# A fused trunk on one core: the four products into the residual take the weights as the moving operand, and the residual is kept with a token to a partition

## The chip, the core and the metric

The kernel is one program on one of the eight cores of a Trainium2 chip. The metric is the device time of one execution in microseconds (us); the time of a kernel is the median of its runs. Of the core's engines five matter here: PE multiplies matrices, DVE, ACT and POOL compute elementwise, and the queue of SP issues nearly all loads from memory.

## What is computed

The batch is one sequence of 256 tokens of width 2048, in float32. Two layers follow each other; each has a mixer and an MLP, and each of these reads the residual `h` through a norm with a scale and a shift that a conditioning vector `c` gives, and adds its result back through a gate:

```python
for i in range(2):
    mod = (silu(c) @ w_mod[i] + b_mod[i])          # 6 x 2048 numbers
    sh1, sc1, g1, sh2, sc2, g2 = split(mod, 6)
    u = rmsnorm(h, norm_mix_g[i]) * (1 + sc1) + sh1
    mix = conformer_conv(u) if i == 0 else mamba2(u)
    h = h + g1 * mix
    u = rmsnorm(h, norm_mlp_g[i]) * (1 + sc2) + sh2
    h = h + g2 * ((relu(u @ w1[i]) ** 2) @ w2[i])  # 2048 -> 8192 -> 2048
return rmsnorm(h, final_norm_g)
```

`conformer_conv` is a product to 4096 columns (pw1), a gate, a causal convolution of 31 taps per channel, a layer norm and a product 2048 to 2048 with a bias (pw2). `mamba2` is a product to 10,304 columns, a short convolution, a scan over two chunks of 128 tokens, a norm and a product 4096 to 2048 (wout). So four products go into the residual: pw2, the w2 of layer 0, wout, and the w2 of layer 1.

## The kernel before

**Tiles.** Activations lie with a channel to a partition: a tile is 128 channels by 256 tokens. The residual `h` is four tiles of [128, 4, 256]. Only within the last MLP it is turned round: `to_rows` transposes `h` into two tiles of [128 tokens, 2048] (`ht`).

**Products.** Weights arrive in tiles of 1 MB (512 rows by 512 columns, `load_w`, three buffers). For precision each is split, in two halves of 128x1024 numbers: ACT casts a half to the high part `wh` (L292), DVE computes the rest `wl` (L293); activations are split the same way and stored side by side (512 columns: 256 high, 256 low). Two ways of multiplying stand in the program:

- `block` (L311 on): the weight is the stationary operand, the activation moves. Per 128x128 piece of weight there is one matmul over 512 columns (`wh` with both parts) and one over 256 (`wl` with the high part): 512 matmuls for four tiles. In the form `single` there are three of 256 columns instead. One *block* is 512 output columns from 2048 input rows, hence four weight tiles.
- `block_t` (L333 on): the activation is stationary, the weight moves, always 512 columns: per 128 rows of weight three matmuls for each half of the tokens (L350 to L352). The result has a token to a partition. Before the change only the w2 of layer 1 uses it.

`outer` runs the first three blocks of an MLP's w1 together, with the norm's output made on the way.

**Into the residual.** `into_acc` adds the partial results of a w2 chunk (there are four chunks `c` of 2048 hidden channels) into accumulators on DVE and ACT; `into_h` multiplies by the gate, a number per partition, and adds to `h` on DVE (L627), and ACT squares the result (L443) for the norm that follows. `rstd_bcast` sums the squares over partitions by PE (L419), takes the root and spreads the result over all partitions by PE (L433). `modulate` then makes the next input `u` with DVE and ACT.

**The conditioning.** The 24,576 numbers of `mod` are 192 dot-product jobs (*gemvs*): a tile of w_mod of 1 MB (`wm<-wmT`) is loaded by SP, and DVE multiplies it by `silu(c)` and sums it (L247, SCALAR_TENSOR_TENSOR `wm`); after each fourth, POOL adds the bias (L255), which completes one tile `mod` of 4 columns. From the first MLP on, the tiles go through a ring of two buffers `wm`. They are streamed beside the products: `pump(n)` starts n jobs of a list at each weight tile, by the lists `RATE_...`; `need(layer, seg)` starts at once whatever of a segment is still in the list. The gate of the MLP is the segment G2. In `mlp(0)` the list is G2 of layer 0 first, then the segments of layer 1.

**What sets the order.** All loads of weights and of w_mod are on the queue of SP and are held in the order in which the program starts them (`stream`). On the engines the order is made by a scheduler from the program's order and priorities: splits of a weight tile are drawn `ahead` by a number of instructions. Small jobs (`todo`) are generators; `step`, called within the products, advances them by one. They use the two PSUM banks `ms`, the products use the six banks `mm`.

Of the kernel before, what the change touches and what calls it, by code (L numbers as in the profile page):

```python
# [15 lines left out]
P = 128  # L16
# [68 lines left out]
def layout(inp):  # L85
# [26 lines left out]
    for l, s, g in PE_GROUPS:  # L112
# [3 lines left out]
        "fg": np.ascontiguousarray(a["final_norm_g"].reshape(1, D)),  # L116
        "xT": np.ascontiguousarray(a["x"][0].T.reshape(4, 4, P, T).transpose(0, 2, 1, 3)),
# [27 lines left out]
class Trunk:  # L145
# [40 lines left out]
    def prologue(self):  # L186
        nc, a = self.nc, self.a
        self.h = [self.b("h", [P, 4, T]) for _ in range(4)]
# [8 lines left out]
        for g in range(4):  # L197
            nc.scalar.dma_start(out=self.h[g], in_=a["xT"][g])
# [134 lines left out]
    def block_t(self, src, rhs, evac):  # L333


        banks = [self.bank(self.mm, "mm") for _ in range(2)]
        mm = self.nc.tensor.matmul
        for g in range(4):
            w = self.load_w(src[g])
            with self.tc.high_priority(self.ahead):  # L340
                parts = self.split_w(w)
            for i, (wh, wl) in enumerate(parts):
                last = g == 3 and i == 1
                order = [(q, k) for q in range(2) for k in range(2)] if last else [
                    (q, k) for k in range(2) for q in range(2)]
                for q, k in order:
# [3 lines left out]
                    mm(banks[q], lhsT=hi, rhs=wh[:, k, :], start=g == 0 and t == 0, stop=False)  # L350
                    mm(banks[q], lhsT=hi, rhs=wl[:, k, :], start=False, stop=False)  # L351
                    mm(banks[q], lhsT=lo, rhs=wh[:, k, :], start=False, stop=g == 3 and t == 3)  # L352
                    if last and k:
                        evac(q, banks[q])
                self.step()
                self.step()

# [88 lines left out]
    def modulate(self, r, layer, sc, sh, g):  # L446

        ug = self.b("u", [P, 4, 2 * T], F32R)
        for t in range(4):
            m = self.t("nrm", [P, T], bufs=2)  # L450
            self.nc.vector.scalar_tensor_tensor(
                out=m, in0=self.h[g][:, t, :], scalar=self.mod_tile(layer, sc, g)[:, t:t + 1],
                in1=r, op0=ALU.mult, op1=ALU.mult)
            self.split_x(ug, t, m, self.mod_tile(layer, sh, g)[:, t:t + 1])
        return ug


    def conformer(self):
        nc, a = self.nc, self.a
        ss = []  # L460
        for g in range(4):
            for t in range(4):
                ss = self.square_sum(ss, self.h[g][:, t, :])
# [4 lines left out]
        def make_u(g):  # L468
            for t in range(4):
                m = self.t("nrm", [P, T], bufs=2)  # L470
                nc.vector.scalar_tensor_tensor(
                    out=m, in0=self.h[g][:, t, :], scalar=self.mod_tile(0, SC1, g)[:, t:t + 1],
# [92 lines left out]
        native([(b, a["pw1"][b]) for b in range(FIRST)], u, glu, before=before)  # L565
# [49 lines left out]
    def into_h(self, st, b, gate, after=None):  # L615
# [9 lines left out]
        def evac(j, parts):  # L625
# [3 lines left out]
            if after:  # L629
                after(4 * b + j, h(j))  # L630
# [427 lines left out]
```

## Time and profile before

| | |
|---|---|
| time, median of 3 runs | 2635.68 us (2634.64 to 2639.17) |
| the profiled execution | 2639.67 us, of which the span of the profile is 2637.9 us |
| PE busy | 2531.5 us, 96% of the span |
| DVE busy | 2038.0 us, 77% |
| ACT busy | 1358.4 us, 51% |
| POOL busy | 193.1 us, 7% |
| read from memory | 652.83 MB |

All times below are in us from the start of the span. The stages lie so: the first norm and pw1 with the convolution to about 345, pw2 to 453, MLP of layer 0 to 1189 (its w1 chunk 0 from 461 to 555.7, its w2 chunk 0 from 555.7 to 646.3), mamba to 1704, wout to 1896, MLP of layer 1 to 2626, the last norm to the end. PE busy counts pipelined matmuls, so it says that PE had work, not that it ran at its peak; the granted clock (PEclk) is the share of full speed that PE was given.

### The profile page before, as it was taken

The page shows a single profiled execution, that of the slowest core. Times are in us where ns is not written, and L with a number is a line of the kernel's source. Part 1 is how long each engine was busy: PE and PEld are TensorE (multiplying, and loading weights), DVE is VectorE, ACT ScalarE, POOL GpSimd, SP SyncE. Part 2 cuts the span into 40 slices and gives each one's busy share as a digit, 9 for nine tenths or more (in the row PEclk, how much of TensorE's full clock was granted, in tenths as well). Part 3 has the DMA queues.
Part 4 walks back from the last instruction along what each step waited for, and adds up shares of the span by engine and source line. Part 5 has one row for each costly group of instructions (what it writes and reads, how often), then busy time and mean ns, then how long its engine had stood idle before and what let it go on. Part 6 is the DMA issues. An engine that isn't in the chain of part 4 may idle for free.

```text
span 2637.9 us, 36706 instructions
## 1 busy us (share of the span) xinstructions
PE 2531.5 (96%) x14359; PEld 2189.4 (83%) x14359; DVE 2038.0 (77%) x2738; ACT 1358.4 (51%) x2141; POOL 193.1 (7%) x189
## 2 busy tenths in 40 slices
PE   4799879999999999999999999999999999999998
PEld 3688469988888888898888888888997888888886
DVE  7799988987888888888877777888865565565565
ACT  2288654454443434446877766744454344443443
POOL 0023310000000000000000000000000101101000
PEclk9899889999999999999999999999999999999999
DMA  9866659788888888874655555688655555555554
GB/s 406 341 251 254 260 215 354 303 318 323 317 313 330 324 321 311 327 302 164 221 183 184 166 194 182 217 298 316 249 187 176 191 192 191 191 181 196 185 190 143
DMA packets 92591, 657.40 MB, mean 249 GB/s; under 512 B 10465, under 2 KB 10465, under 8 KB 14465
## 3 DMA queue, kind: packets, MB, share of 16 engines
q1 hardware_dynamic: 88274, 640.73, 66.3%
q0 software_dynamic: 3136, 10.59, 1.3%
q10 hardware_dynamic: 1008, 3.75, 0.4%
q8 instruction: 112, 1.84, 0.3%
q14 instruction: 61, 0.50, 0.1%
HBM read 652.83 MB, written 2.20 MB: 248 GB/s over the span
## 4 chain that ended last, share of the span: by engine, by line
PE 86%; DVE 9%; DMA 2%; issue 2%; ACT 1%; POOL 0%; ACTq 0%; SPq 0%; DVEq 0%; POOLq 0%
PE mm L300 69%; PE mm L352 4%; PE mm L351 4%; PE mm L350 4%; DVE taps L503 3%; DVE taps L506 2%; DMA hid<-wmT 2%; DVE hid L247 1%; PE mm L546 1%; DVE wm L247 1%; PE ms L972 1%; DVE wl L293 0%; PE ms L433 0%; DMA h<-xT 0%; PE ms L419 0%
## 5 line engine op out<-in xcount | busy, mean ns | idle before, releaser
L300 PE MATMUL mm<-u,wh 128*128 128x512 f32 (+1 forms) x4544 | 1378.2, 366 | 4.0 <-ACT u L401 1.9
L292 ACT CAST wh<-w 128x1024 fp32r<-128x1024 f32 x768 | 806.7, 1050 | 1027.4 <-PE mm L300 732.8
L293 DVE TENSOR_TENSOR wl<-w,wh 128x1024 fp32r<-128x1024 f32 x768 | 942.4, 1229 | 461.0 <-ACT wh L292 455.6
L300 PE MATMUL mm<-u,wl 128*128 128x256 f32 x3840 | 1083.4, 283 | 0.1
L300 PEld LDWEIGHTS mm<-u,wh 128*128 128x128 f32 x4544 | 815.3, 191 | 149.5 <-issue 3.4
L300 PEld LDWEIGHTS mm<-u,wl 128*128 128x128 f32 x3840 | 731.5, 191 | 3.8 <-issue 1.7
L300 PE MATMUL mm<-hid,wh 128*128 128x512 f32 (+1 forms) x1344 | 455.6, 389 | 2.8 <-DVE acc L644 2.8
L300 PE MATMUL mm<-hid,wl 128*128 128x256 f32 x1280 | 360.4, 282 | 0.0
L247 DVE SCALAR_TENSOR_TENSOR wm<-wm,scb 128x2048 f32<-128x2048 f32 x135 | 308.9, 2288 | 2.3 <-DMA wm<-wmT 2.3
L300 PEld LDWEIGHTS mm<-hid,wh 128*128 128x128 f32 x1344 | 249.0, 189 | 60.5 <-DVE acc L644 3.1
L546 PE MATMUL mm<-u,w 128*128 128x256 f32 x1024 | 230.2, 389 | 21.3 <-ACT u L474 21.3
L300 PEld LDWEIGHTS mm<-hid,wl 128*128 128x128 f32 x1280 | 242.6, 190 | 0.2 <-issue 0.2
L546 PEld LDWEIGHTS mm<-u,w 128*128 128x128 f32 x1024 | 199.8, 196 | 51.5 <-ACT u L474 23.0
L352 PE MATMUL mm<-wh,hid 128*128 128x512 f32 x512 | 199.9, 391 | 0.0
L350 PE MATMUL mm<-wh,hid 128*128 128x512 f32 x512 | 199.9, 390 | 0.0
L351 PE MATMUL mm<-wl,hid 128*128 128x512 f32 x512 | 199.5, 390 | 0.0
L497 ACT ACTIVATE taps<-u,par 128x256 f32<-128x256 f32 x360 | 148.6, 499 | 19.6 <-DVE u L488 10.5
L255 POOL TENSOR_TENSOR mod<-mod,par 128x4 f32<-128x4 f32 x48 | 52.5, 1094 | 1080.3 <-DVE wm L247 880.5
L247 DVE SCALAR_TENSOR_TENSOR hid<-hid,scb 128x2048 f32<-128x2048 f32 x49 | 113.9, 2329 | 14.9 <-ACT scb L202 11.2
L352 PEld LDWEIGHTS mm<-wh,hid 128*128 128x128 f32 x512 | 96.2, 188 | 19.7
L350 PEld LDWEIGHTS mm<-wh,hid 128*128 128x128 f32 x512 | 96.2, 188 | 19.7
L351 PEld LDWEIGHTS mm<-wl,hid 128*128 128x128 f32 x512 | 96.2, 188 | 19.5
(197 smaller groups left out, 1623.9 us busy)
## 6 DMA issues: line engine op xcount, KB each, us to landing
w<-w SPq DMA_DIRECT2D x256, 1024.0 KB, 4.9
wm<-wmT SPq DMA_DIRECT2D x137, 1024.0 KB, 7.2
w<-win SPq DMA_DIRECT2D x80, 1024.0 KB, 4.9
hid<-wmT SPq DMA_DIRECT2D x55, 1024.0 KB, 8.3
w<-pw SPq DMA_DIRECT2D x48, 1024.0 KB, 5.1
w<-wout SPq DMA_DIRECT2D x32, 1024.0 KB, 6.3
acc<-ac_d POOLq DMA_DIRECT2D x16, 512.0 KB, 7.2
h<-xT ACTq DMA_DIRECT2D x4, 512.0 KB, 13.1
```

Source lines behind the costliest of these rows:

```text
L247: nc.vector.scalar_tensor_tensor(out=w, in0=w, scalar=1.0, in1=self.scb, op0=ALU.mult, op1=ALU.mult, accum_out=m[:, i:i + 1])
L255: nc.gpsimd.tensor_tensor(out=m, in0=m, in1=self.col("b_mod", (layer * 6 + seg) * NT + 4 * kg, 4), op=ALU.add)
L292: nc.scalar.copy(out=wh, in_=w[:, s, :])
L293: nc.vector.tensor_tensor(out=wl, in0=w[:, s, :], in1=wh.bitcast(F32), op=ALU.subtract)
L300: mm = lambda out, lhsT, rhs, **kw: self.nc.tensor.matmul(out, lhsT=lhsT, rhs=rhs, skip_group_check=True, **kw)
L350: mm(banks[q], lhsT=hi, rhs=wh[:, k, :], start=g == 0 and t == 0, stop=False)
L351: mm(banks[q], lhsT=hi, rhs=wl[:, k, :], start=False, stop=False)
L352: mm(banks[q], lhsT=lo, rhs=wh[:, k, :], start=False, stop=g == 3 and t == 3)
L497: nc.scalar.activation(out=p4[:, q, :], in_=vp[:, k + q:k + q + T], func=AF.Identity, scale=self.col("w_dw", ct * TAPS + k + q), bias=self ...
L503: nc.vector.tensor_add(wide, wide, p4)
L506: nc.vector.scalar_tensor_tensor(out=o, in0=vp[:, k:k + T], scalar=self.col("w_dw", ct * TAPS + k), in1=o, op0=ALU.mult, op1=ALU.add)
L546: nc.tensor.matmul(o, lhsT=w[:, t, j * P:(j + 1) * P], rhs=rhs[g][:, t, :], start=g == 0 and t == 0 and j < 2, stop=g == 3 and t == 3, ski ...
```

## The change

- `h` is two tiles [128 tokens, 2048] from the start. They are loaded from a second copy of the input with tokens as rows (`a["x"]`), by the queue of SP among the loads of pw1. The transposed input stays for the first norm alone (`xT`, in the buffers `acc`).
- pw2, the w2 of layer 0 and wout use `block_t` too. `block_t` takes a list of weight tiles, a `pump`, and banks that are kept open over two calls: of wout the first half of the rows is done for three blocks (six open banks), then the second half for these, then both halves of the fourth.
- `into_rows` does the evacuation for all four: DVE multiplies a bank by the gate as rows and POOL adds it to `h`; where the residual is complete after it (pw2, wout, the last chunk of a w2), DVE adds and ACT squares and sums.
- `gate_rows` makes the gate as rows in all partitions: `row` multiplies the gate column, broadcast as stationary operand, by the identity, 4 calls of 128 columns for each 512 numbers, into a bank `ms` that ACT copies out. In pw2 a second such set carries gate times bias, and DVE adds it to `h`. In the MLP of layer 0 `need(layer, G2)` and `gate_rows` now stand after the w1 chunk 0, ahead of the w2 chunk 0.
- A norm (`normed`) is a sum of the squares' sums, root and reciprocal for each token, DVE and ACT scale the rows into two tiles, and `modulate` transposes them back by PE, 32 transposes of 128x128 in a norm, and applies scale and shift from PSUM on ACT and DVE. `to_rows` and, for the three norms concerned, `rstd_bcast` are gone.

```diff
-    def block_t(self, src, rhs, evac):
-        banks = [self.bank(self.mm, "mm") for _ in range(2)]
+    def block_t(self, srcs, rhs, evac, pump=None, banks=None, done=True):
+        first = banks is None
+        banks = banks or [self.bank(self.mm, "mm") for _ in range(2)]
...
+    def normed(self, sq):
+        nc = self.nc
+        r = self.t("rcol", [P, 2])
+        nc.vector.reduce_sum(out=r, in_=sq, axis=mybir.AxisListType.X)
+        nc.scalar.activation(out=r, in_=r, func=AF.Sqrt, scale=1.0 / D, bias=self.eps)
+        nc.vector.reciprocal(r, r)
+        x = [self.b("hid", [P, D]) for _ in range(2)]
+        for g in range(4):
+            s = slice(g * 512, (g + 1) * 512)
+            for q in range(2):
+                if g and q:
+                    nc.scalar.mul(out=x[q][:, s], in_=self.h[q][:, s], mul=r[:, q:q + 1])
+                else:
+                    nc.vector.tensor_scalar_mul(out=x[q][:, s], in0=self.h[q][:, s], scalar1=r[:, q:q + 1])
+        return x
+
+    def modulate(self, x, layer, sc, sh, g):
...
+        for i in range(2):
+            ps = self.bank(self.ms, "ms")
+            for t in range(2):
+                ct = 4 * g + 2 * i + t
+                for q in range(2):
+                    nc.tensor.transpose(ps[:, t * T + q * Q:t * T + (q + 1) * Q],
+                                        x[q][:, ct * P:(ct + 1) * P], self.ident)
+            for t in range(2):
...
+                nc.scalar.activation(out=ug[:, k, :T], in_=v, func=AF.Identity, scale=c, bias=o)
+                m = self.t("nrm", [P, T], bufs=2)
+                nc.vector.tensor_scalar(out=m, in0=v, scalar1=c, scalar2=o, op0=ALU.mult, op1=ALU.add)
+                nc.vector.tensor_tensor(out=ug[:, k, T:], in0=m, in1=ug[:, k, :T].bitcast(F32), op=ALU.subtract)
...
+        for q in range(2):
+            self.stream(self.h[q], a["x"][q])
...
-            self.block(a["pw2"][b], v, self.into_h(st, b, gate), pump=pump, single=True)
+        self.todo.append(self.gate_rows(0, G1, gb))
+        for b in range(4):
+            self.block_t(a["pw2"][b], v, self.into_rows(b, True), pump=pump)
...
+    def row(self, ps, cols):
+        for j in range(4):
+            self.nc.tensor.matmul(ps[:, j * P:(j + 1) * P], lhsT=cols[:, j:j + 1].broadcast_to([P, P]),
+                                  rhs=self.ident, start=True, stop=True)
...
-            if layer == 1:
-                for b in range(4):
-                    self.block_t(a["w2"][layer, c, b], hid, self.into_rows(b, c == 3))
-                continue
+            if c == 0:
+                self.need(layer, G2)
+                self.todo.append(self.gate_rows(layer, G2))
             for b in range(4):
-                if c == 3:
-                    self.need(layer, G2)
-                ev = self.into_h(st, b, gate, after) if c == 3 else self.into_acc(st, b, c == 0)
-                self.block(a["w2"][layer, c, b], hid, ev, pump=pump, single=c == 3 and b == 3)
+                self.block_t(a["w2"][layer, c, b], hid, self.into_rows(b, c == 3, finish), pump=pump)
...
-        for b in range(4):
-            self.block(a["wout"][0, b], self.out_hl[:4], self.into_acc(st, b, True), pump=pump)
+        half = lambda i, b, **kw: self.block_t(a["wout"][i, b], self.out_hl[4 * i:4 * i + 4], self.into_rows(b, True),
+                                               pump=pump, **kw)
+        open_ = [half(0, b, done=False) for b in range(3)]
         while self.todo:
             self.step()
-        self.need(1, G1)
-        for b in range(4):
-            self.block(a["wout"][1, b], self.out_hl[4:], self.into_h(st, b, gate), pump=pump, single=b == 3)
-        self.need(1, SC2, SH2)
+        for b in range(3):
+            half(1, b, banks=open_[b])
+        half(1, 3, banks=half(0, 3, done=False))
+        self.need(1, SC2, SH2, G2)
```

How the order of instructions moves is shown at three places, all at the passage from the w1 to the w2 of chunk 0 in the MLP of layer 0.

The queue of SP, before: `w_564` and `w_570` are the last two weight tiles of w1, `w_588` and `w_594` the first two of w2; each `wm` is one tile of w_mod.

```order
L277 DMA w_564_4088<-w 128x2048
L277 DMA wm_4090<-wmT 128x2048
L277 DMA w_570_4133<-w 128x2048
L277 DMA w_588_4208<-w 128x2048
L277 DMA wm_4210<-wmT 128x2048
L277 DMA w_594_4253<-w 128x2048
```

The queue of SP, now: `w_570` is again the last tile of w1, `w_596` the first of w2.

```order
L279 DMA w_570_3788<-w 128x2048
L279 DMA wm_3859<-wmT 128x2048
L279 DMA wm_3862<-wmT 128x2048
L279 DMA wm_3866<-wmT 128x2048
L279 DMA wm_3870<-wmT 128x2048
L279 DMA wm_3873<-wmT 128x2048
L279 DMA wm_3876<-wmT 128x2048
L279 DMA wm_3880<-wmT 128x2048
L279 DMA wm_3884<-wmT 128x2048
L279 DMA wm_3887<-wmT 128x2048
L279 DMA wm_3890<-wmT 128x2048
L279 DMA w_596_3896<-w 128x2048
```

Ten loads of w_mod, which are the rest of segment G2, now stand between the last tile of w1 and the first of w2; in the queue before there is none at this place. In return ten loads of w_mod are gone from the end of wout.

DVE, now, at the same passage: `wm` rows are gemvs, `a` and `hid` rows the rest of the evacuation of the last w1 block, the `wl` row the first split of w2.

```order
L249 SCALAR_TENSOR_TENSOR wm_3866,mod_3868<-wm_3866,scb 128x2048
L411 TENSOR_TENSOR hid_3818<-a_3844,hid_3818 128x256
L720 SCALAR_TENSOR_TENSOR a_3855<-lo_3852 128x256
L249 SCALAR_TENSOR_TENSOR wm_3870,mod_3868<-wm_3870,scb 128x2048
L411 TENSOR_TENSOR hid_3818<-a_3855,hid_3818 128x256
L249 SCALAR_TENSOR_TENSOR wm_3873,mod_3868<-wm_3873,scb 128x2048
L249 SCALAR_TENSOR_TENSOR wm_3876,mod_3868<-wm_3876,scb 128x2048
L249 SCALAR_TENSOR_TENSOR wm_3880,mod_3882<-wm_3880,scb 128x2048
L249 SCALAR_TENSOR_TENSOR wm_3884,mod_3882<-wm_3884,scb 128x2048
L249 SCALAR_TENSOR_TENSOR wm_3887,mod_3882<-wm_3887,scb 128x2048
L249 SCALAR_TENSOR_TENSOR wm_3890,mod_3882<-wm_3890,scb 128x2048
L295 TENSOR_TENSOR wl_3903<-w_596_3896,wh_3902 128x1024
```

The first two of the ten gemvs (`wm_3859`, `wm_3862`) come just ahead of the evacuation of the last w1 block; the third, the first row here, stands behind the reads of all four banks of that block, and the first split of w2 behind the tenth. Before, the first tile of w2 was split ahead of that evacuation.

PE, now, at the start of the w2 chunk 0: `ms` rows are `gate_rows`, `mod` the finished gate columns.

```order
L302 MATMUL mm_3654<-u_3377,wh_3794 128x512
L302 MATMUL mm_3654<-u_3377,wl_3795 128x256
L654 MATMUL ms_3930<-ident,mod_3701 128x128 x4
L654 MATMUL ms_3949<-ident,mod_3868 128x128 x4
L654 MATMUL ms_3955<-ident,mod_3882 128x128 x4
L358 MATMUL mm_3894<-wh_3902,hid_3453 128x512
L358 MATMUL mm_3895<-wh_3902,hid_3453 128x512
L359 MATMUL mm_3894<-wl_3903,hid_3453 128x512
```

Three of the four groups of gate rows stand between the last matmul of w1 and the first of w2; before, the two followed each other directly.

197 lines of the change are left out of this document (81 added, 116 removed).

## The prediction

> **What bounds the kernel now.** I read the page first, the engines' busy time and the chain of waits:
>
> ```profile
> PE 2531.5 (96%) x14359; PEld 2189.4 (83%) x14359; DVE 2038.0 (77%) x2738; ACT 1358.4 (51%) x2141; POOL 193.1 (7%) x189
> PE 86%; DVE 9%; DMA 2%; issue 2%; ACT 1%; POOL 0%; ACTq 0%; SPq 0%; DVEq 0%; POOLq 0%
> ```
>
> PE has work nearly always and holds 86% of the chain. So a matmul less counts in full, and so does every new wait of PE. Which holds where is read from the windows by stage (busy time per engine, then granted clock, share of the DMA engines, GB/s):
>
> ```profile
> core 0: us, PE busy (x) PEld busy (x) DVE busy (x) ACT busy (x) POOL busy (x), PEclk, DMA share, GB/s
> 357.00:400.00 43.00, 42.18 (x325) 41.89 (x326) 39.72 (x70) 27.02 (x47) 1.12 (x1) 0.91 0.73 276
> 400.00:453.40 53.40, 53.40 (x446) 53.21 (x444) 47.99 (x56) 21.95 (x28) 2.63 (x4) 1.00 0.95 361
> 453.40:461.40 8.00, 3.30 (x22) 2.88 (x21) 6.54 (x12) 4.08 (x8) 0.00 (x0) 0.71 0.78 295
> 461.40:555.70 94.30, 94.30 (x705) 91.31 (x706) 85.76 (x113) 46.60 (x72) 6.53 (x5) 0.97 0.81 305
> 555.70:646.30 90.60, 90.60 (x515) 78.61 (x514) 72.81 (x82) 40.38 (x54) 3.35 (x3) 1.00 0.87 321
> 1098.50:1189.40 90.90, 90.90 (x577) 81.73 (x575) 79.59 (x103) 39.67 (x52) 3.75 (x5) 1.00 0.80 303
> 1704.00:1804.90 100.90, 98.10 (x572) 84.42 (x571) 86.86 (x118) 47.02 (x66) 4.59 (x5) 0.98 0.81 301
> 1804.90:1895.80 90.90, 90.90 (x577) 81.77 (x575) 80.63 (x101) 38.09 (x46) 3.35 (x3) 1.00 0.80 305
> 1895.80:1902.20 6.40, 4.08 (x29) 3.60 (x29) 4.37 (x11) 3.63 (x8) 0.00 (x0) 0.88 0.48 172
> 1902.00:1999.00 97.00, 97.00 (x732) 94.04 (x731) 58.85 (x89) 50.35 (x80) 0.00 (x0) 0.97 0.48 163
> 1999.00:2093.30 94.30, 93.09 (x418) 74.92 (x417) 52.04 (x64) 37.70 (x42) 11.45 (x6) 1.00 0.56 190
> 2183.70:2270.80 87.10, 87.10 (x386) 72.13 (x386) 47.64 (x50) 35.62 (x38) 10.60 (x6) 1.00 0.57 193
> ```
>
> Each product into the residual fills PE: in both halves of pw2 (357 to 453.4), in the w2 chunks of layer 0 (555.7 to 646.3 is chunk 0, 1098.5 to 1189.4 chunk 3) and in wout (1704 to 1895.8) the busy time is the window or close to it. The last row is a w2 chunk of layer 1, which already uses `block_t`: 87.1 us for the work that takes `block` 90.6. PE is not full in the passages between stages, 453.4 and 1895.8, where the norm's chain runs.
>
> **The change part by part: the four products.** `block` and `block_t` are compared by these rows: four blocks cost 90.6, 90.9 where one of them is `single`, and 87.1 in the new form. The gain is 90.6 - 87.1 = 3.5 us for each of the w2 chunks 0 to 2 of layer 0, 10.5; chunk 3 gives 90.9 - 87.1 = 3.8; wout 3.5 and 3.8 in its two halves (100.9 holds other small matmuls, which stay), 7.3. In pw2 all four blocks are single, each 0.3 dearer by the difference above: 90.6 + 1.2 - 87.1 = 4.7. Sum **-26.3**. It depends on DVE keeping up. In layer 0 and wout it is busy 73 to 87 us of a chunk; in pw2 39.72 + 47.99 = 87.7, which is more than the new 87.1. There the gain is the least sure, from 0 to 4.7.
>
> **Gate rows and `to_rows`.** The nearest rows are those of `to_rows` in the MLP of layer 1:
>
> ```profile
> L717 PE MATMUL ms<-diag,ones 128*128 128x128 f32 x32 | 7.2, 306 | 1.2 <-DVE diag L716 1.2
> L705 PE MATMUL ms<-ident,h 128*128 128x128 f32 x32 | 5.3, 293 | 0.7 <-ACT wm L706 0.7
> ```
>
> The 16 float32 calls of the gate (two records each, x32) fall into the window 1999.0 to 2093.3, which is 94.3 - 87.1 = 7.2 us longer than one without: 0.45 us a call with the wait for DVE, each alone among other matmuls. The 32 transposes fall into 1902 to 1999, 97.0 - 94.3 = 2.7 longer than the same stage of layer 0: 0.084 each. By their own row, 5.3 + 0.7, it would be 0.19. A gate call now is of the same size, but four follow each other and none waits for a diagonal from DVE. So its cost lies between two such records, 2 x 0.084 = 0.17, and 0.45; I take 0.25, nearer the first, because transposes also come in fours. pw2 has 32 calls: 8.0. The MLP of layer 0 has 16; four stand before the last w1 block, 1.0, and twelve in the stall below. wout has 16: 4.0. In layer 1 16 calls, 4.0, replace the 7.2 + 2.7 of `to_rows`: -5.9. Sum **+7.1** (+4 to +20). The ACT copies and the eight DVE additions of pw2 lie beside PE, but the second set of a group waits for a bank that DVE frees. If that cover fails, 8 x 0.69 = 5.5 us are added.
>
> **Transposes of the norms.** 32 in each of three norms, 0.084 to 0.19: 2.7 to 6.0 a norm; I take 3.3, since the difference of windows is wall time. PE is full from the first matmul of each stage on, so nothing hides them. Sum **+10** (8 to 18).
>
> **The norm's chain.** How long the new chain is, the end of the kernel shows, which has it already:
>
> ```profile
> 2625.90 0.69 DVE L734 TENSOR_TENSOR t<-mm,h 128x512 f32<-128x512 f32 x1
> 2626.63 0.69 DVE L738 TENSOR_TENSOR wm<-wm,t 128x512 f32<-128x512 f32 x1
> 2627.24 0.68 DVE L740 TENSOR_TENSOR wm<-wm,h 128x512 f32<-128x512 f32 x1
> 2627.35 0.63 ACT L739 ACTIVATE t<-wm 128x512 f32<-128x512 f32 x1 [0.64 <-DVE wm L738]
> 2628.72 0.15 DVE L1026 TENSOR_REDUCE rcol<-mom 128x2 f32<-128x8 f32 x1
> 2628.91 0.29 ACT L1027 ACTIVATE rcol<-rcol,eps 128x2 f32<-128x2 f32 x1 [0.83 <-DVE rcol L1026]
> 2629.24 0.17 DVE L1028 RECIPROCAL rcol<-rcol 128x2 f32<-128x2 f32 x1 [0.36 <-ACT rcol L1027]
> ```
>
> From the last matmul to the reciprocal 3.5 us, of which L740's multiplication by the last norm's weight delays some 0.6 that the middle norms lack; then one scaling of a half's 512 columns, 0.7 like L740, the first transposes at half clock, some 0.9, and an ACT pass of 0.5. That is 5 to 6 us against 8.0 at 453.4 and 6.4 at 1895.8. **-2** for the three (-5 to +3).
>
> **The ten gemvs.** This decides. The order of the queue of SP shows ten loads of w_mod between the last w1 tile and the first w2 tile of chunk 0, and the ring has two buffers: each load waits for the gemv two before it. What such a load and its work cost, and when they stood there before:
>
> ```profile
> L247 DVE SCALAR_TENSOR_TENSOR wm<-wm,scb 128x2048 f32<-128x2048 f32 x135 | 308.9, 2288 | 2.3 <-DMA wm<-wmT 2.3
> L255 POOL TENSOR_TENSOR mod<-mod,par 128x4 f32<-128x4 f32 x48 | 52.5, 1094 | 1080.3 <-DVE wm L247 880.5
> w<-w SPq DMA_DIRECT2D x256, 1024.0 KB, 4.9
> wm<-wmT SPq DMA_DIRECT2D x137, 1024.0 KB, 7.2
> ```
> ```profile
> 521.44 0.42 SPq L277 DMA_DIRECT2D wm<-wmT  x1
> 527.20 0.43 SPq L277 DMA_DIRECT2D wm<-wmT  x1
> 532.80 6.15 SPq L277 DMA_DIRECT2D w<-w  x2
> ```
> ```profile
> 534.03 2.29 DVE L247 SCALAR_TENSOR_TENSOR wm<-wm,scb 128x2048 f32<-128x2048 f32 x1
> 539.52 2.29 DVE L247 SCALAR_TENSOR_TENSOR wm<-wm,scb 128x2048 f32<-128x2048 f32 x1
> 549.93 2.52 DVE L293 TENSOR_TENSOR wl<-w,wh 128x1024 fp32r<-128x1024 f32 x2
> 555.14 0.75 DVE L393 TENSOR_TENSOR lo<-mm,lo 128x256 f32<-128x256 f32 x2
> 556.48 2.28 DVE L247 SCALAR_TENSOR_TENSOR wm<-wm,scb 128x2048 f32<-128x2048 f32 x1
> ```
>
> In the clock of before: the two gemvs ahead of the ten end at 536.3 and 541.8, so loads 1 and 2 issue then. In DVE's order gemv 1 stands behind the last split of w1, which at 549.93 is the first of the two and stood behind a gemv that now comes after it; so it starts at about 548.5, and gemvs 1 and 2 end at 550.8 and 553.1. Loads 3 and 4 land 5 us later, but gemv 3 stands behind the reads of the last w1 block's four banks, whose last matmul ends at 555.7. It runs from about 556.6 to 558.9. Only then load 5 issues. From there the ring alone paces: a load of 4.9 and a gemv of 2.3 make 7.3 us for each buffer, two buffers by turns. Load 5 at 559.0, 7 at 566.3, 9 at 573.6; load 6 at 562.1, 8 at 569.4, 10 at 576.7. The load of the first w2 tile is the next on the queue and issues at 577.1. Gemv 10 runs from 581.7 to 584.0, POOL's 1.1 follow, and the gate rows that wait for it stand on PE ahead of the first w2 matmul. The w2 tile, landing by 583 to 584, needs 1.05 us on ACT and its split, behind gemv 10 on DVE, 1.2. PE goes on at about 586: a stall of 30.3 us. It then runs at half clock for some time: after the 8.0 us gap at 453.4 the mean clock of the next 94.3 us is 0.97, so 2.8 us are lost. Sum **+33**. Bounds: if the evacuation did not stand in the way, ten loads at 7.3/2 from 536.4 would end at 573, and gemv and gate would let PE go on at 575.5: +20 and restart. With 7.2 for each load (the median beside others) the cycle is 9.5 and PE goes on at 592: +36 and restart. So +22 to +39. Waiting behind are DVE's splits and, through PE, everything else: nothing covers it. The ten gemvs that are missing later in wout free DVE for 10 x 2.3 us there, where PE is the bound: 0.
>
> **The rest.** Two loads of 1 MB for `h` in the convolution's stage, and the start of pw2 with gate rows among its first matmuls: +1 (0 to 5).
>
> The sum is -26.3 + 7.1 + 10 - 2 + 33 + 1 = **+22.8 us**. On the profiled execution, 2639.67, that gives 2662.5; it lies 4.0 above the median of the runs, 2635.68, to which the forecast is related: **2658**.
>
> **Rivals.** *The ten loads are hidden* (the other side). They are on the queue 23 us before PE needs the first w2 tile, and the row of 400 to 453.4 moves 361 GB/s, by which ten tiles take 29 us; with loads running ahead the stall would be near nothing. Then the sum is -10.2 and the time 2625.5. It decides from the point where the ring keeps both buffers loading while DVE evacuates. Against it: two buffers only, and gemv 3 behind that evacuation in DVE's order. Chance 0.08. *Stall at its lower bound and cheap rows*: +22 for the stall, gate rows and transposes at their lower ends, -26.3 + 4 + 8 - 3 + 22 = +5, no change that can be told: 0.07. *DVE becomes the bound in pw2*: 87.7 us of work before, and it now also adds bias rows; the gain of 4.7 is lost and 5.5 added: 2668. Chance 0.13. *The w2 chunks become bound by transfers*: at 87.1 us chunk 0 would need 321 x 90.6/87.1 = 334 GB/s; the row with 361 at a DMA share of 0.95 speaks against a limit there. If it is one, 10.5 are lost: 2669. Chance 0.05. The Trainium skill, page "DMA: Bandwidth & Descriptors", section "Specifications", gives some 358 GB/s from memory for a core; by that too the stage would fit, narrowly.
>
> *The clock does not come back through transposes.* In the three passages PE starts with transposes, interleaved with matmuls; if the clock stays at half until matmuls alone have run, the 3.3 us of transposes are spent at half clock and delay its return: 3 x 3.3 = +10 at most, 2668. For it: 0.71 and 0.88 granted in the passages. Against: transposes come eight at a time among matmuls. Chance 0.07. The Trainium skill says so in "TensorE: Matmul & The Clock Gate", section "Part 4: PE-mode transpose": work in transpose mode does not count as activity. No row here has a passage that starts with transposes, so the trace can neither agree nor disagree.
>
> **How the numbers follow.** The forecast has 0.60, the rivals 0.08, 0.07, 0.13, 0.05 and 0.07. The cases on the slow side lie within 2640 to 2676, by the stall's bounds (-11, +6) and those of gate rows and transposes (-5, +12), not all at once; the range is 2638 to 2676 and leaves out the hidden case and the far ends. Changes under 0.2%, 5.3 us, can't be told from none. Faster: the hidden case and a little of the low one, 0.10. Same: 0.07. Slower: 0.83.
>
> **What would show it.** Right: in the window from the last w1 to the first w2 matmul of chunk 0 PE idles some 30 us, ended by POOL's `mod` or by DVE, with eight or more `wm` loads issued 3 to 5 us apart; w2 chunks 1 to 3 take 87 to 88 us, the halves of wout 3 to 4 us less; the passages last 5 to 7 us and the stages after them are 3 us longer. Wrong: PE busy through that window, w2 chunks at 90 us, or a stall as long in pw2 or wout. The sum fails above all if the order on the queue of SP is not what paces the ten loads.

## The result and the profile after

The changed kernel takes 2669.76 us (median of 4 runs, 2669.64 to 2670.33), the kernel before 2637.03 us beside it (4 runs, 2634.64 to 2639.17). The ratio is 1.0125 with a 95% interval of 1.0107 to 1.0142: slower by 32.7 us. The forecast was 2658, slower by 22, with a range of 2638 to 2676. Between the two profiled executions the spans differ by 30.0 us (2637.9 and 2667.9); the profiled execution of before lies 2.6 us above its median.

The busy times and the chain of waits of the changed kernel:

```profile
PE 2526.6 (95%) x13211; PEld 2139.9 (80%) x13211; DVE 2023.5 (76%) x2578; ACT 1352.8 (51%) x2104; POOL 226.5 (8%) x213
PE 73%; DVE 3%; ACT 1%; issue 1%; DMA 0%; ACTq 0%; POOL 0%; DVEq 0%
```

PE has 5 us less of work and the span is 30 us longer, so PE waits more than before. Where it does, the windows by stage show (columns as before: PE, PEld, DVE, ACT, POOL busy, granted clock, DMA share, GB/s):

```profile
356.10:454.50 98.40, 97.97 (x448) 80.59 (x448) 87.48 (x115) 50.95 (x76) 2.83 (x5) 0.97 0.80 314
454.50:463.10 8.60, 2.06 (x9) 1.59 (x9) 5.86 (x13) 5.52 (x10) 0.00 (x0) 0.72 0.51 193
463.10:560.50 97.40, 96.59 (x739) 92.96 (x739) 92.45 (x122) 47.67 (x73) 2.12 (x6) 0.99 0.74 280
560.50:591.90 31.40, 4.70 (x25) 4.21 (x24) 21.96 (x26) 4.88 (x10) 0.40 (x2) 0.56 0.82 313
591.90:682.80 90.90, 89.65 (x387) 73.16 (x387) 75.34 (x65) 34.34 (x35) 21.97 (x15) 0.98 0.90 352
951.30:1038.60 87.30, 87.30 (x387) 72.27 (x386) 73.88 (x72) 35.66 (x38) 14.74 (x13) 1.00 0.85 333
1216.60:1224.60 8.00, 2.17 (x9) 1.59 (x9) 7.34 (x14) 6.03 (x12) 0.00 (x0) 0.68 0.34 131
1733.40:1921.80 188.40, 186.43 (x860) 153.25 (x858) 129.00 (x141) 81.83 (x99) 4.81 (x6) 0.99 0.70 258
1921.80:1929.10 7.30, 1.99 (x10) 1.57 (x9) 5.65 (x13) 5.29 (x10) 0.00 (x0) 0.79 0.40 144
1929.10:2032.50 103.40, 98.12 (x732) 93.67 (x732) 60.64 (x90) 48.13 (x73) 0.00 (x0) 0.98 0.44 153
2032.30:2123.00 90.70, 90.70 (x417) 75.62 (x416) 48.01 (x50) 37.67 (x42) 10.62 (x6) 1.00 0.53 186
```

The fourth row is the passage from the w1 to the w2 of chunk 0 in the MLP of layer 0, where before the last matmul of w1 was followed directly by the first of w2: 31.4 us, in which PE does only the gate rows. That one row is more than the 30.0 us between the two spans. The w2 chunk at 951.3 takes 87.3 us in place of 90.6, as forecast. And one stage is longer that should not be: the first stage of the MLP of layer 1 (1929.1 to 2032.5) takes 103.4 us, of which PE is busy 98.1; before, it took 97.0 and PE was busy all of it.

The stall in detail. The loads on the queue of SP, the work of DVE with what ended its idle time, and POOL's last addition for the gate, and what PE and ACT wait for at the end:

```profile
546.90 35.47 SPq L279 DMA_DIRECT2D wm<-wmT  x10
582.47 0.38 SPq L279 DMA_DIRECT2D w<-w  x1
```
```profile
562.47 2.28 DVE L249 SCALAR_TENSOR_TENSOR wm<-wm,scb 128x2048 f32<-128x2048 f32 x1
570.07 2.29 DVE L249 SCALAR_TENSOR_TENSOR wm<-wm,scb 128x2048 f32<-128x2048 f32 x1 [2.08 <-DMA wm<-wmT]
577.23 2.29 DVE L249 SCALAR_TENSOR_TENSOR wm<-wm,scb 128x2048 f32<-128x2048 f32 x1 [2.32 <-DMA wm<-wmT]
584.71 2.29 DVE L249 SCALAR_TENSOR_TENSOR wm<-wm,scb 128x2048 f32<-128x2048 f32 x1 [2.69 <-DMA wm<-wmT]
587.54 2.29 DVE L249 SCALAR_TENSOR_TENSOR wm<-wm,scb 128x2048 f32<-128x2048 f32 x1 [0.53 <-DMA wm<-wmT]
591.09 2.36 DVE L295 TENSOR_TENSOR wl<-w,wh 128x1024 fp32r<-128x1024 f32 x2 [1.25 <-ACT wh L294]
```
```profile
589.92 0.20 POOL L257 TENSOR_TENSOR mod<-mod,par 128x4 f32<-128x4 f32 x1 [14.73 <-DVE wm L249]
590.17 2.08 PE L654 MATMUL ms<-ident,mod 128*128 128x128 f32 x8 [12.85 <-POOL mod L257]
590.01 1.99 ACT L294 CAST wh<-w 128x1024 fp32r<-128x1024 f32 x2 [12.07 <-DMA w<-w]
```

The ten loads take from 546.9 to 582.4 to issue, the first w2 tile follows at 582.47. The gemvs that use one and the same buffer start at 562.47, 570.07, 577.23 and 584.71, so 7.6, 7.2 and 7.5 us apart: a load and its gemv, as the working had it (7.3). DVE is idle between them, waiting for the load. After the tenth, POOL's addition at 589.92 lets PE make the last group of gate rows, and the first w2 matmul starts at 591.9. The w2 tile itself, last in the queue, is no earlier: ACT's first cast of it starts at 590.01 and ends at 591.1. So the gate rows hold PE by some 0.8 us more than the tile does. The prediction put the stall at 30.3 us and it is 31.4.

### The profile page after: what moved, and what is told of

Same layout as the page of the kernel before. It is cut to its first block, busy times and chain, and to the rows that moved or that the text cites. A ratio compares the mean times of both kernels' runs of the same rounds, so it can differ in the third digit from the quotient of the medians.

```text
span 2667.9 us, 34215 instructions
## 1 busy us (share of the span) xinstructions
PE 2526.6 (95%) x13211; PEld 2139.9 (80%) x13211; DVE 2023.5 (76%) x2578; ACT 1352.8 (51%) x2104; POOL 226.5 (8%) x213
## 4 chain that ended last, share of the span: by engine, by line
PE 73%; DVE 3%; ACT 1%; issue 1%; DMA 0%; ACTq 0%; POOL 0%; DVEq 0%
PE mm L302 40%; PE mm L359 10%; PE mm L360 10%; PE mm L358 10%; DVE wl L295 1%; DVE wm L249 1%; PE ms L965 1%; ACT wh L294 0%; PE ms L654 0%; PE ms L934 0%; DVE t L685 0%; PE ms L944 0%; DMA t<-eac_d 0%; PE ms L954 0%; PE ms L481 0%
## 5 line engine op out<-in xcount | busy, mean ns | idle before, releaser
L302 PE MATMUL mm<-u,wh 128*128 128x512 f32 (+1 forms) x3712 | 1189.9, 377 | 5.5 <-DVE u L490 3.1
L302 PE MATMUL mm<-u,wl 128*128 128x256 f32 x3328 | 933.7, 282 | 0.5 <-DVE wl L295 0.5
L302 PEld LDWEIGHTS mm<-u,wh 128*128 128x128 f32 x3712 | 674.7, 189 | 142.4 <-DVE u L490 4.2
L302 PEld LDWEIGHTS mm<-u,wl 128*128 128x128 f32 x3328 | 629.8, 189 | 4.4 <-issue 1.7
L359 PE MATMUL mm<-wl,hid 128*128 128x512 f32 x1152 | 450.1, 391 | 1.9 <-DVE wl L295 1.9
L358 PE MATMUL mm<-wh,hid 128*128 128x512 f32 x1152 | 450.3, 392 | 0.0
L360 PE MATMUL mm<-wh,hid 128*128 128x512 f32 x1152 | 449.5, 390 | 0.0
L359 PEld LDWEIGHTS mm<-wl,hid 128*128 128x128 f32 x1152 | 217.1, 188 | 48.8 <-DVE wl L295 4.2
L360 PEld LDWEIGHTS mm<-wh,hid 128*128 128x128 f32 x1152 | 217.0, 188 | 45.4
L358 PEld LDWEIGHTS mm<-wh,hid 128*128 128x128 f32 x1152 | 216.9, 188 | 45.3 <-issue 0.6
L249 DVE SCALAR_TENSOR_TENSOR hid<-hid,scb 128x2048 f32<-128x2048 f32 x49 | 112.8, 2307 | 15.1 <-ACT scb L204 11.3
L358 PE MATMUL mm<-wh,u 128*128 128x512 f32 x256 | 101.2, 395 | 1.9 <-ACT u L410 1.9
L360 PE MATMUL mm<-wh,u 128*128 128x512 f32 x256 | 100.9, 394 | 0.3 <-DVE u L411 0.3
L359 PE MATMUL mm<-wl,u 128*128 128x512 f32 x256 | 100.8, 394 | 0.0
```

What stands on the lines that cost most here:

```text
L249: nc.vector.scalar_tensor_tensor(out=w, in0=w, scalar=1.0, in1=self.scb, op0=ALU.mult, op1=ALU.mult, accum_out=m[:, i:i + 1])
L302: mm = lambda out, lhsT, rhs, **kw: self.nc.tensor.matmul(out, lhsT=lhsT, rhs=rhs, skip_group_check=True, **kw)
L358: mm(banks[q], lhsT=hi, rhs=wh[:, k, :], start=first and g == 0 and t == 0, stop=False, **kw)
L360: mm(banks[q], lhsT=lo, rhs=wh[:, k, :], start=False, stop=end and k == 1, **kw)
```

## The experiments

**The stall taken away.** The changed kernel, with the gate of the MLP of layer 0 asked for group by group:

```diff
-            if c == 0:
+            if c == 0 and layer == 1:
                 self.need(layer, G2)
                 self.todo.append(self.gate_rows(layer, G2))
             for b in range(4):
+                if c == 0 and layer == 0:
+                    self.need(layer, G2, kg=b)
+                    self.todo.append(self.gate_rows(layer, G2, only=b, wait=8))
```

> The changed kernel, but in the MLP of layer 0 the gate rows are made group by group: group b is needed only before block b of the w2 chunk 0, and its rows are made half a block later, so that the ten loads are not started at once. Theory (the burst of ten gemvs is the stall and the restart at half clock after it): the 31.4 us between the last w1 and the first w2 matmul go to 0 to 1 and the chunk from 90.9 to some 87.3, so the time falls by 33 to 36 us, to 2634 to 2637. Rival (the gates are late anyway, since their gemvs have to be done: PE then waits inside blocks 1 to 3 for the gate rows): a stall of 10 us or more stays, 2645 or more. Rival (the stall hid other work, as evacuation and transfers, which now shows): w2 chunk 0 takes 92 us or more, 2640 to 2645.

Measured: 2636.37 us (10 runs, 2633.74 to 2638.29), with 2637.21 for before beside it, ratio 0.9997 (0.9988 to 1.0006). The stall is gone, and the w2 chunk 0 follows w1 at once:

```profile
560.60:650.90 90.30, 90.30 (x411) 75.01 (x410) 76.80 (x76) 37.05 (x41) 14.99 (x9) 1.00 0.86 334
```

33.4 us are back, as the theory had it. The chunk takes 90.3 us and not 87.3, since it now holds the gate rows that stood in the stall before: x411 against x387 records, 24 more or twelve calls. No wait of PE over 1 us remains in that MLP. So the rest of the change, without the burst, is worth nothing that can be measured: -0.8 us against before, with an interval on both sides of no change.

**The burst alone.** The kernel before, with one line moved, so that products and norms stay as they were:

```diff
+            if c == 0:
+                self.need(layer, G2)
             for b in range(4):
-                if c == 3:
-                    self.need(layer, G2)
```

> The kernel before with one line moved: the rest of segment G2 of layer 0 is asked for ahead of the w2 chunk 0 and not of chunk 3; products, norms and gates stay. Theory (the queue of SP: ten loads stand ahead of the first w2 tile, and the ring of two paces them): PE idles 27 to 31 us between w1 and w2 of chunk 0, with no gate row on PE there, and the time is 2637 + 29 + 3 = 2665 to 2671. Rival (PE's gate rows, which wait for POOL in PE's order, make the stall, not the loads): under 5 us of stall, 2637 to 2642.

Measured: 2664.93 us (4 runs, 2663.52 to 2665.48), ratio 1.0104 (1.0089 to 1.0119), 27.7 us above before and just below the range given.

```profile
555.30:584.30 29.00, 0.04 (x1) 0.00 (x0) 19.70 (x25) 3.14 (x8) 0.40 (x2) 0.56 0.80 303
584.30:676.20 91.90, 91.84 (x513) 79.94 (x514) 71.89 (x73) 39.49 (x48) 7.31 (x9) 0.97 0.91 354
```

PE idles 29.0 us, though there are no gate rows in this kernel and PE waits for no POOL there. The queue of SP and the ring of two buffers are enough. The 31.4 of the changed kernel are 2.4 more. Of these, 0.8 lie behind the tenth gemv: from its end to the first w2 matmul it is 1.2 us here and 2.1 there, where gate rows stand between. The other 1.6 are there before; here the ten loads also begin earlier, 19.4 us ahead of the end of w1 (at 535.88) in place of 13.6 (at 546.90).

**Six gemvs in place of ten.** The changed kernel, where the last group of the gate is asked for only at block 3 of the w2 chunk 0:

```diff
+                if c == 0 and layer == 0 and b in (0, 3):
+                    self.need(layer, G2, kg=b or 2)
+                    for k in (range(3) if b == 0 else (3,)):
+                        self.todo.append(self.gate_rows(layer, G2, only=k, wait=8 if k == 3 else 0))
```

> The changed kernel with a burst of six gemvs in place of ten: the fourth group of the gate in the MLP of layer 0 is asked for at block 3 of the w2 chunk 0 only. Theory (the ring of two buffers paces the burst, 7.3 us for a pair): four gemvs less take 14.6 us off the stall, so PE idles 16 to 18 us and the time is 2654 to 2656. Rival (a transfer rate or a latency that does not depend on their number sets the stall): PE idles over 25 us, or the stall falls by DVE's work alone, 4 x 2.3 = 9 us, to 22.

Measured: 2653.39 us (4 runs, 2652.17 to 2654.72), ratio 1.0054 (1.0040 to 1.0068), just below the range given.

```profile
560.50:576.80 16.30, 2.54 (x16) 2.35 (x15) 12.64 (x18) 4.18 (x9) 0.20 (x1) 0.60 0.83 326
```

The stall is 31.4 - 16.3 = 15.1 us shorter for four gemvs less, 3.8 each. That is half a round of load and gemv (7.2 to 7.6), not DVE's 2.3. So the ring's pace is shown for two buffers; a ring of more was not run.

**The wait in the MLP of layer 1.** What made the first stage there 103.4 us long, the groups of PE between 1900 and 2130 show, in the changed kernel (busy, mean ns of one, idle before and what ended it):

```profile
L302 PE MATMUL mm<-u,wh 128*128 128x256 f32 (+1 forms) x469 | 103.0, 310 | 5.3 <-DVE u L490 2.9 <-ACT u L487 2.4
L481 PE MATMUL ms<-ident,hid 128*128 128x128 f32 x32 | 5.7, 313 | 5.3 <-DVE hid L469 5.3
L654 PE MATMUL ms<-ident,mod 128*128 128x128 f32 x32 | 4.0, 274 | 0.0
```

PE waits 5.3 us for the norm's output `u` within the stage. The transposes of a row group stand on PE directly ahead of the matmuls that use them, and between the two lie a pass of ACT and two operations of DVE. The experiment lets the group after be made earlier (on top of the version without the burst, in the MLP of layer 1):

```diff
+        ready = [make(0)] if early else []
         for g in range(4):
-            x = make(g)
+            x = ready[g] if early else make(g)
             for b, src in enumerate(srcs):
+                if early and b == 1 and g < 3:
+                    ready.append(make(g + 1))
```

> The kernel of e1_groups, and in the MLP of layer 1 the transposes and the input u of row group g+1 are made while group g still has two of its three weight tiles to multiply. Theory (in that stage PE waits three times some 1.8 us for u, since its transposes stand on PE directly ahead of the matmuls that use it): 103.4 us of that stage become 97.5 to 99, and the time is 4 to 6 us below e1_groups. Rival (transposes and gate rows themselves make the stage longer, not the wait): within 1.5 us of e1_groups.

Measured: 2629.66 us (9 runs, 2628.70 to 2631.58), ratio 0.9970 (0.9960 to 0.9980), 6.7 us below the version without it, a little more than expected.

```profile
1894.80:1991.30 96.50, 96.50 (x730) 93.34 (x730) 60.46 (x90) 47.94 (x73) 0.00 (x0) 0.98 0.46 164
```

The stage takes 96.5 us and PE is busy all of it. The wait was the reason, not the transposes: all 32 are still there. Of the 6.9 us that the stage lost, 5.3 are the idle time above; what the rest is, no run separates.

**The norm's chain, and the splits within it.** The prediction added up the chain's own operations. In the changed kernel, before the MLP of layer 1, there stands one thing more:

```profile
1922.58 0.68 DVE L689 TENSOR_TENSOR h<-h,t 128x512 f32<-128x512 f32 x1
1923.17 1.22 DVE L295 TENSOR_TENSOR wl<-w,wh 128x1024 fp32r<-128x1024 f32 x1
1924.31 0.69 DVE L689 TENSOR_TENSOR h<-h,t 128x512 f32<-128x512 f32 x1
1925.03 0.63 ACT L690 ACTIVATE t<-h 128x512 f32<-128x512 f32 x1 [1.01 <-DVE h L689]
1926.31 0.17 DVE L461 RECIPROCAL rcol<-rcol 128x2 f32<-128x2 f32 x1 [0.36 <-ACT rcol L460]
1927.14 2.06 PE L481 MATMUL ms<-ident,hid 128*128 128x128 f32 x8 [5.31 <-DVE hid L469]
```

A split of a weight tile, 1.22 us, runs between the two additions to `h`, so the second comes 1.1 us later. In the passage after pw2 two splits stand so. The experiment holds all splits that come after a norm behind its first two scalings, on top of e5_look:

```diff
+    def behind(self, ins):
+        if self.chain is not None:        # the norm's scaling of q = 1 in the first columns
+            self.tc.add_manual_dep(ins.ins, self.chain.name, mybir.DependencyInfo(
+                mybir.DependencyClass.NoSync, mybir.DependencyReason.DATA), reason="behind")
...
-            nc.vector.tensor_tensor(out=wl, ...)
+            self.behind(nc.vector.tensor_tensor(out=wl, ...))
```

> The kernel of e5_look, and on DVE the splits of the weight tiles that come after a norm are held behind the first two scalings of the rows, so that no split of 1.22 us stands within the norm's chain. Theory (the splits make the three passages longer than the chain alone): from the last matmul to the first one after, 8.6, 8.0 and 7.2 us become some 6.7, 7.0 and 6.1, and the time falls by 3 to 5 us below e5_look. Rival (the splits held back are then missing at the first matmuls, so the wait only moves): within 1.5 us of e5_look.

Measured: 2637.98 us (10 runs, 2636.90 to 2640.53), ratio 0.9999 (0.9990 to 1.0008): 8.3 us *slower* than e5_look, which ran in another group (before took 2638.63 in this one and 2637.21 in that). The passage and the stage after it, before the MLP of layer 1:

```profile
1894.00:1899.70 5.70, 1.94 (x8) 1.52 (x8) 4.37 (x11) 5.12 (x11) 0.00 (x0) 0.80 0.00 0
1899.70:1999.40 99.70, 97.25 (x729) 93.94 (x730) 63.05 (x93) 48.04 (x73) 0.00 (x0) 0.96 0.48 170
```

The passage is shorter, 5.7 in place of 7.3, and the one after pw2 6.6 in place of 8.6; the one before mamba is not, with 8.4 in place of 8.0. And the stages after them are longer by more: 99.7 in place of 96.5 here, 102.5 in place of 97.5 in the MLP of layer 0. What PE waits for there are not the splits themselves:

```profile
1900.64 2.35 DVE L296 TENSOR_TENSOR wl<-w,wh 128x1024 fp32r<-128x1024 f32 x2
1902.91 0.41 DVE L502 TENSOR_TENSOR u<-nrm,u 128x256 fp32r<-128x256 f32 x1
1903.38 0.58 PE L303 MATMUL mm<-u,wh 128*128 128x256 f32 x1 [2.44 <-DVE u L502]
```

The splits that were held back now stand on DVE among the operations that make `u`, and PE waits 2.44 us for `u`. The theory held for two passages of three and its conclusion was wrong; the rival's "the wait only moves" was too mild. In a variant only the splits of the later tiles are held back, those of the first may stand in the chain:

```diff
+                self.hold = g > 0 or b > 0          # not for the first tile of the stage
```

> e7_order, but the splits of the first weight tile of each stage may again stand within the norm's chain; those of later tiles may not. Theory (e7_order lost because the first matmuls then waited for their own splits, while splits of later tiles in the chain only lengthen it): the passage before the MLP of layer 1 falls from 7.2 to some 6.1 without a new wait, that before mamba from 8.0 to 7.3, and the time is 1 to 2 us below e5_look, 2627.5 to 2628.7. Rival (any split that is held back is missed later): at or above e5_look, 2629.5 or more.

Measured: 2628.67 us (5 runs, 2625.63 to 2629.72), ratio 0.9962 (0.9950 to 0.9975). Against e5_look, which ran in another group of runs, the intervals overlap; whether it gains 1 us stays open. The passage before the MLP of layer 1 is 6.1 us as expected, but the stage after it is 97.3 in place of 96.5, and the passage before mamba is 8.0 as it was.

**Gate rows of the bias in pw2.** In e5_look pw2 takes 98.4 us. Is PE or DVE the bound there? The second set of gate rows is replaced: the bias is loaded as rows, and POOL multiplies and adds.

```diff
-                    ps = self.bank(self.ms, "ms")
-                    self.row(ps, plus[g])
+                    nc.gpsimd.tensor_tensor(out=plus[g], in0=plus[g], in1=v[:, k, :], op=ALU.mult)
                     for q in range(2):
-                        nc.vector.tensor_add(h, ps, h)
+                        nc.gpsimd.tensor_tensor(out=h, in0=h, in1=plus[g], op=ALU.add)
```

> The kernel of e5_look without the second set of gate rows in pw2: the bias is loaded as rows and POOL multiplies it by the gate and adds it to h, so that PE has 16 float32 calls less there and DVE eight additions less. Theory (pw2 is bound by PE, and a call costs what it does in the MLP of layer 1, 3.5 us for 16): pw2 goes from 98.4 to some 95, and the time falls by 3 to 4 us below e5_look. Rival (DVE is the bound in pw2, as the prediction's third rival had it): by the additions, 8 x 0.69, it falls by 5 us or more. Rival (POOL's additions are late for the evacuation, or neither engine bounds the stage): within 1 us, or slower.

Measured: 2629.93 us (5 runs, 2629.26 to 2631.61), ratio 0.9967 (0.9955 to 0.9979), the same as e5_look. pw2 is longer, 102.2 us, with a wait of 4.2 for a split. The reason stands in DVE's rows, while POOL works on `acc` and `h`:

```profile
381.67 4.53 DVE L296 TENSOR_TENSOR wl<-w,wh 128x1024 fp32r<-128x1024 f32 x2
386.13 1.27 DVE L696 TENSOR_TENSOR t<-mm,acc 128x512 f32<-128x512 f32 x2
387.33 0.68 DVE L700 TENSOR_TENSOR h<-h,t 128x512 f32<-128x512 f32 x1
390.16 1.77 DVE L700 TENSOR_TENSOR h<-h,t 128x512 f32<-128x512 f32 x1
391.86 3.38 DVE L250 SCALAR_TENSOR_TENSOR wm<-wm,scb 128x2048 f32<-128x2048 f32 x1
```
```profile
382.85 2.27 POOL L683 TENSOR_TENSOR acc<-acc,acc 128x512 f32<-128x512 f32 x1
385.20 3.96 POOL L686 TENSOR_TENSOR h<-h,acc 128x512 f32<-128x512 f32 x2
389.12 3.97 POOL L683 TENSOR_TENSOR acc<-acc,acc 128x512 f32<-128x512 f32 x2
```

Beside POOL a split takes 2.27 us (two in 4.53) in place of 1.22, an addition 1.77 in place of 0.68, a gemv 3.38 in place of 2.28. The operation that reads one operand from PSUM (`t<-mm,acc`) keeps its 0.64 (two in 1.27). Not every other one is slower: the addition at 387.33 took 0.68, though POOL worked beside it. To show that POOL is the cause, the same twelve operations were put on DVE:

```diff
-                    nc.gpsimd.tensor_tensor(out=plus[g], in0=plus[g], in1=v[:, k, :], op=ALU.mult)
+                    nc.vector.tensor_mul(plus[g], plus[g], v[:, k, :])
                     for q in range(2):
-                        nc.gpsimd.tensor_tensor(out=h, in0=h, in1=plus[g], op=ALU.add)
+                        nc.vector.tensor_add(h, h, plus[g])
```

> e8_bias with its twelve operations (gate times bias, and its addition to h) on DVE and none of them on POOL. Theory (in e8_bias each DVE operation that ran beside one of POOL's took up to twice its time, 2.3 us in place of 1.22 for a split, so that a split came 4.2 us late for PE; POOL's work is the cause): the splits take 1.2 us again, the wait of 4.2 us inside pw2 is gone, pw2 takes some 95 us (98.4 less 16 calls of 0.22) and the time is 2625 to 2627. Rival (DVE has no room in pw2, whoever does the additions): PE waits for splits by 2 us or more, and the time is 2629 to 2632.

Measured: 2623.51 us (5 runs, 2619.14 to 2624.57), ratio 0.9941 (0.9928 to 0.9955), somewhat better than expected.

```profile
355.60:450.00 94.40, 94.06 (x416) 77.22 (x416) 90.35 (x120) 50.33 (x76) 6.52 (x5) 0.97 0.84 327
L296 DVE TENSOR_TENSOR wl<-w,wh 128x1024 fp32r<-128x1024 f32 x31 | 37.5, 1220 | 2.7 <-ACT wh L295 2.6
```

DVE has twelve operations *more*, and pw2 takes 94.4 us in place of 102.2; the splits are at 1.22 us again. So POOL's work was the cause, and PE is the bound of pw2: 16 calls less took 4.0 us off 98.4.

**Both together**, held splits and the bias by POOL, as a candidate before the causes were known:

> e7_order and e8_bias together, as the candidate for a version faster than both kernels. If the two edits are independent, the gains against e5_look add up: 6 to 9 us, 2621 to 2624. If the passage after pw2 takes back what pw2 gains, the gain of the larger one alone stays.

Measured: 2639.31 us (11 runs, 2638.60 to 2641.51), ratio 1.0004 (0.9996 to 1.0013). That is e7_order's time within 1.3 us: neither edit had a gain to add, and the 2621 to 2624 expected were not met.

The version that beats both kernels is e11_bias_dve: gate groups spread over the chunk, the next group's norm output made ahead, and the bias as rows on DVE. It is 14.5 us below the kernel before that ran beside it (2638.02), and 46 us below the changed kernel, which ran in another group.

## Why the prediction was right, and where its sum was short

The sign, the mechanism and the place were right, and the range held the time. The sum said +22.8, against +30.0 between the profiled executions. Step by step:

| step of the prediction | predicted | measured in the trace | from |
|---|---|---|---|
| the four products | -26.3 | about -25 | chunks of w2 at 87.3 to 87.9; wout 188.4 - 191.8, less 16 calls of gate rows; pw2 98.4 - 96.2, less 32 calls |
| gate rows and `to_rows` | +7.1 | +5 | a call is (90.7 - 87.2)/16 = 0.22, taken 0.25; in layer 1 `to_rows` had cost more than the calls do |
| transposes within the stages | +10 | +5 | 24 of 32 lie in each stage; 97.4 - 94.4 with four calls, so 2.1 in the MLP of layer 0 |
| the norm's chain (three passages) | -2 | +3.2 | 8.0, 6.3, 6.4 before; 8.6, 8.0, 7.3 now |
| the ten gemvs, with the restart | +33 | +35 | 31.4 + 0.2 that matmuls overlapped before, and 90.9 - 87.3 = 3.6 in the chunk after it, where PE idles 1.25 and some 1.5 go to the half clock, granted until about 595 |
| the rest | +1 | 0 | start of pw2 -1.1, other stages +1 |
| not foreseen: the wait for `u` in layer 1 | | +7 | 103.4 less the 96.5 of e5_look |

The mechanism of the ten gemvs was right where it counts, in the queue and the ring: the burst alone gives 29.0 us, six gemvs 16.3, none no stall. Of the bounds given for it, neither end was needed. Two of its parts stood in the order as foreseen but decided little. The evacuation held gemv 3 by 1.0 us at most: its load, issued at 556.65, had landed at 561.47, and it started at 562.47. And the first split of w2 waited at the end for ACT's cast, hence for the tile, and not for gemv 10, which was done at 589.8. The first two loads issued some 5.5 us later than the working had them (546.90 and 552.06, against 536.3 and 541.8 in the clock of before, whose w1 ends 4.8 us earlier). This changed little, because gemv 1 stands behind the last split of w1 anyway: it started at 554.33, 1.0 us later than taken, and the stall is 1.1 us longer.

Two steps failed, in the sum rather than in its sign. "**PE is full from the first matmul of each stage on, so nothing hides them**" treated the transposes of the norms as work alone. In the MLP of layer 1 they are a dependence, PE to ACT to DVE and back to PE, once for each row group, and on PE the matmuls that need the result came next. That cost 7 us, more than the transposes themselves. In layer 0 there was no such wait, and the window has PE idle only 0.8 us: there the transposes came in fours, the first at 465.4, 2.3 us after the stage began, where in layer 1 one stands at 1932.8 and seven together at 1948.3, 19 us after it began and directly ahead of their use. Why they come earlier there was not tried. "**5 to 6 us against 8.0**" took the end of the kernel as a model of the chain, where no work of a next stage competes for DVE. In the middle of the kernel splits stand between its parts. (The -2 also did not follow from its own figures: three passages of 5 to 6 us in place of 20.7 in all make -3 to -6.) e7_order shows that the splits stood there for a reason: without them two of the passages are 1.6 and 2.0 us shorter, and the three stages after them longer by 3 to 5.

Of the rivals: the hidden ten loads did not happen, nor did a stall at its lower bound of 20 us. DVE as the bound of pw2 is refuted by the changed kernel, where PE is busy 97.97 of 98.4 us, and by e11_bias_dve, where DVE does 90.4 us of work in 94.4 and PE is still the bound. A limit of transfers in the w2 chunks is refuted for what was asked of it: 87.3 us at 333 GB/s. And no later return of the clock after transposes can be seen, though here the profile needs a second look. Before, the first matmul of the MLP of layer 0 was at 461.4; now it is at 463.05, with eight transposes from 461.04 on. The windows there, before and then now (the granted clock is the third number from the end):

```profile
466.00:467.00 1.00, 1.00 (x7) 1.00 (x6) 0.04 (x1) 0.04 (x1) 0.00 (x0) 0.50 0.00 0
467.00:468.00 1.00, 1.00 (x10) 1.00 (x10) 0.00 (x0) 1.00 (x1) 0.00 (x0) 1.00 0.00 0
```
```profile
463.00:465.00 2.00, 1.76 (x7) 1.42 (x7) 1.69 (x4) 1.02 (x2) 0.00 (x0) 0.50 0.00 0
465.00:467.00 2.00, 2.00 (x19) 2.00 (x19) 2.00 (x5) 1.51 (x3) 0.00 (x0) 0.97 0.03 8
```

Full clock came 5.6 us after the first matmul before, and 2.1 now. The prediction said that no row of before has a passage that starts with transposes; one has. Before the MLP of layer 1 eight transposes of `to_rows` stand at 1900.15 and 1901.44, directly ahead of the first matmul at 1902.21 (so its row for that stage held 24 transposes and not 32), and full clock came 5.2 us after that matmul. Over ten passages with eight transposes ahead, in six kernels, it came after 2.1 to 5.2 us; over the two without, after 5.5 and 5.6. No loss by them can be seen, and more can't be read from so few. The Trainium skill has it in "TensorE: Matmul & The Clock Gate", section "Part 4: PE-mode transpose", that transposes do not count as activity. These traces do not bear out that it costs time here.

## What to carry to other kernels

When code moves the point at which something is *asked for*, look at the order of the queue that serves it before counting any matmul: a burst on a queue that keeps its order costs its length, here a load and its use (7.2 to 7.6 us) for every two tiles of a ring of two, and everything behind it waits. Where a transform of data is moved to the bound engine, ask what must come back from other engines before that engine can go on, and put other work of that engine between; two weight tiles were enough here. And a split or copy that stands in a critical chain may be there for a wait that comes after it; shorten the chain only together with what it prepares.

## What the runs showed of the hardware

DVE operations that read two operands from SBUF can lose time beside POOL: in e8_bias a DVE split of 128x1024 took 2.27 us in place of 1.22, an addition 1.77 in place of 0.68, a gemv 3.38 in place of 2.28, and an operation with one operand in PSUM kept its 0.64. The loss is some 1.1 us each time, however long the operation is, and the addition at 387.33 lost nothing while POOL's `h<-h,acc` beside it (387.32 to 389.16) took 1.84 us in place of the 1.36 that the fastest of these eight took. That looks like taking turns and not like both running slower; no run isolates it. Over pw2 the mean of a split was 1.43 us in place of 1.22:

```profile
L296 DVE TENSOR_TENSOR wl<-w,wh 128x1024 fp32r<-128x1024 f32 x31 | 43.8, 1428 | 5.9 <-ACT wh L295 5.9
```

The Trainium skill, "Advanced Engine Details and Errata", section "GPSIMD Details", says that POOL shares a read and a write interface with DVE and conflicts with DVE instructions that have two SBUF inputs; the rows agree, and give the size. POOL was busy 32.7 of 102.2 us in that stage and still not a free place for elementwise work: moving twelve operations from POOL *to* the busier engine made the stage 7.8 us shorter.
